# A hybrid attention and recurrence layer on one core: the last head's norm taken for both halves at once, attention's first query products ahead of its transposes, and query and key copies ahead of their remainders

## The chip, the cores and the metric

The kernel runs on one core of one Trainium2 chip, in one launch. The metric is the time of one execution in microseconds (us); lower is better. The engines are called as in the profile: PE is the matrix engine (matmuls and transposes, results in the accumulation banks, PSUM), DVE the vector engine, ACT the scalar engine, POOL the general-purpose engine, and SP the engine whose queue issues most transfers. Each engine carries out its own instructions strictly in the order in which they were written down; between engines they wait on semaphores.

## The reference

One layer of a bidirectional encoder over 1024 tokens of width 1024 (plus 16 learned meta tokens), cut to what matters here:

```python
a = rms_norm(h, norm_mix[l])
(q_na, k_na, v_na, q_hg, z_f, z_b, i_hg, g_hg, gate_na, gate_hg) = split_cols(a @ w_in[l])
y_na = neighbourhood_attention(hd(q_na), hd(k_na), hd(v_na), na_rpb[l]).reshape(B, L, NA_WIDTH) @ w_na_out[l]
y_hg = hgrn2_branch(q_hg, z_f, z_b, i_hg, g_hg, lb_all[:, l], hg_norm[l]) @ w_hg_out[l]
mix = jax.nn.sigmoid(gate_na) * y_na + jax.nn.sigmoid(gate_hg) * y_hg
h = h + mix @ w_o[l]
...
# the end of hgrn2_branch: o is (B, L, heads, 128)
o = o * lax.rsqrt(jnp.mean(o * o, axis=-1, keepdims=True) + EPS)
o = o.reshape(B, L, HG_VDIM) * gain * jax.nn.silu(g)
...
# neighbourhood_attention: 8 heads of 64, a window of 8 x 16 tokens of the grid, and the meta keys
p = softmax([q . k_window * scale + bias, q . k_meta * scale]);  out = p . [v_window, v_meta]
```

## The kernel before

The layer runs as a sequence of stages on one core: the first norm and the transposition of the tokens (`start`), four heads of the recurrence (`hgrn`, one call for each head `hd`), four pairs of attention heads (the loop over `p`), the two gates and the two output projections, and the MLP. All products are made to near-float32 accuracy by splitting each operand into a rounded high part and a remainder (`hi` and `lo`): `mm3` issues three matmuls for one product, lines L122, L123 and L124, so a projection of 128 columns from 1024 features over 512 tokens is 8 x 3 = 24 matmuls.

`proj(col, evac, meta_evac)` makes one block of 128 columns of the input projection. For a query block it runs in two pieces of 512 tokens. For a key or value block (which also need the 16 meta tokens) it runs in three: 256 tokens, 256 tokens with the 16 meta tokens (272 columns), and 512 tokens. Each piece has an accumulation bank of its own, all named `mm` in the profile, and `evac` copies it out. `mm_tile` hands these banks out in a cycle of three: two from the pool `mm`, one from the pool `mx`. So a piece waits until the piece three places earlier has been copied out.

The end of a recurrence head stands behind the `yield` of `hgrn`. Its output lies in two accumulation banks `po`, one for each half of the tokens (`hf` = 1, then 0). For each half: ACT squares it (`sq`), DVE sums the squares (`ss`), POOL makes the reciprocal root in two instructions (`st`, `hrs`; helper `rsqrt_mean`, L92 and L93), DVE scales (`on`), PE transposes the four 128-blocks (`opt`, L490), DVE applies gain and gate (`ot`), and SP writes `ot` to memory. Before the change DVE does one half to its end before it begins the other.

Attention takes two heads of 64 as a pair, stacked in 128 partitions. `ev_q` copies a query piece into two tiles `QX0` and `QX1` (index `i`): ACT writes the rounded copy of head `i` into its 64 partitions (L749), DVE the remainder into the other 64 (L750). `ev_k` does so for the keys: ACT writes the rounded copy twice into `KS0` or `KS1` (L757 and, shifted by 64 partitions, L758), DVE the remainder into `KL0` or `KL1` (L759). `mev_k` does the same for the meta keys (L766 to L768). After the value projection come the scores (`nsc`, L799 and L800), their softmax (`pr`: DVE L805, ACT L807, DVE L808 and L809), the transposes of the probabilities (`ppt`, L820 and L822) copied out as `PT`, and the products with the values (`pov`). The projection matmuls of the next pair fill PE between them. Meanwhile POOL adds the bias into the mask (`NB`, L742) and makes sums of the tokens for a later stage (`rt`, L187 and L191).

The weight block of a projection is loaded into `raw`, and split by ACT into `hi` (L112, or L115 with a scale) and by DVE into `lo` (L113 or L116), one block ahead of its use. `hi` and `lo` have two buffers each.

The start of the layer is recorded in the order in which it is written (`manual_schedule`). From the first recurrence head to the end of the gates a scheduler sets the order on each engine, so the order on an engine can differ from the order of the source: it already moves the first query projection of attention in between the last head's products.

## Time and profile before

| | |
|---|---|
| time, median of 3 runs | 1529.9 us (1528.22 to 1530.62) |
| time of the profiled execution | 1530.97 us |
| its span from the first to the last instruction | 1529.2 us |
| PE busy in the span | 1503.1 us (98%) |
| DVE, ACT, POOL busy | 1034.4, 657.4, 377.6 us |
| the recurrence ends, attention begins | about 334 to 347 us from the start |
| the four attention pairs | about 343 to 576 us |

The profiled execution took 1.77 us more than its span, and 1.07 us more than the median. PE is busy nearly all the time, so what an edit can win is a stretch in which PE stands idle. A row of the timeline gives the start of an instruction and its duration in us, the engine, the line of the kernel, the operation, what it writes and reads, and the shapes; in square brackets stands how long the engine was idle before it and what ended that wait. Matmuls overlap: the next one starts before the modelled end of the last.

### The profile page before, as it was taken

What the parts mean: (1) busy time and instruction counts of PE and PEld (TensorE: products, weight loads), DVE (VectorE), ACT (ScalarE), POOL (GpSimd) and SP (SyncE); (2) the same over time, 40 slices, a digit from 0 to 9 for tenths busy, and PEclk for the clock granted to TensorE, in tenths of its full rate; (3) what the DMA queues carried; (4) which work ended last, traced back from release to release, by engine and by line L of the source; (5) the groups of instructions that cost most, each with busy time, mean ns of one, the idle gap of its engine ahead of it and who ended that gap; (6) DMA issues with size and microseconds to landing.
All of it is one profiled execution on the core that took longest, in us unless ns stands there. A gap on an engine that the chain in (4) does not pass through costs nothing.

```text
span 1529.2 us, 23532 instructions
## 1 busy us (share of the span) xinstructions
PE 1503.1 (98%) x9236; PEld 1255.8 (82%) x9236; DVE 1034.4 (68%) x1608; ACT 657.4 (43%) x1168; POOL 377.6 (25%) x355
## 2 busy tenths in 40 slices
PE   9999999999999999999999999999999999999998
PEld 8888888878888887887888887888888888888886
DVE  7876566645786777666475358877777544877876
ACT  6131313126665576334133235455555533434444
POOL 3313130324404400011000122444444200231142
PEclk9999999999999999999999999999999999999999
DMA  4201011113222227435756123544444576563324
GB/s 168 59 29 57 28 57 29 48 47 108 80 68 94 95 68 244 132 130 172 248 165 220 53 86 117 177 154 153 152 151 158 208 261 234 193 234 110 96 83 152
DMA packets 142591, 195.61 MB, mean 128 GB/s; under 512 B 8192, under 2 KB 90240, under 8 KB 142480
## 3 DMA queue, kind: packets, MB, share of 16 engines
q1 hardware_dynamic: 133216, 172.53, 34.3%
q10 hardware_dynamic: 7088, 14.24, 2.4%
q0 software_dynamic: 2176, 7.34, 1.3%
q8 instruction: 72, 1.18, 0.3%
q14 instruction: 39, 0.32, 0.1%
HBM read 139.56 MB, written 54.53 MB: 127 GB/s over the span
## 4 chain that ended last, share of the span: by engine, by line
PE 89%; DVE 5%; issue 2%; ACT 2%; DMA 1%; POOL 0%; POOLq 0%; ACTq 0%; SPq 0%; DVEq 0%
PE mm L122 11%; PE mm L123 10%; PE mm L124 10%; PE mm L1372 5%; PE pa L1372 4%; PE pb L879 4%; PE pb L880 4%; PE pb L881 4%; PE pb L1372 4%; PE pc L1372 4%; PE pc L879 3%; PE pc L881 3%; PE pc L880 3%; PE pa L879 2%; PE pa L880 2%
## 5 line engine op out<-in xcount | busy, mean ns | idle before, releaser
L122 PE MATMUL mm<-aT,hi 128*128 128x512 f32 (+2 forms) x600 | 214.7, 358 | 2.8 <-DVE QX L750 1.5
L124 PE MATMUL mm<-aT,lo 128*128 128x512 f32 (+2 forms) x600 | 212.2, 354 | 0.0
L123 PE MATMUL mm<-aT,hi 128*128 128x512 f32 (+2 forms) x600 | 211.2, 352 | 0.0
L97 DVE TENSOR_TENSOR dl<-ur,dh 128x1024 fp32r<-128x1024 f32 x54 | 71.1, 1316 | 87.3 <-ACT dh L96 85.3
L96 ACT CAST dh<-ur 128x1024 fp32r<-128x1024 f32 x54 | 56.9, 1054 | 166.4 <-issue 91.1
L122 PEld LDWEIGHTS mm<-aT,hi 128*128 128x128 f32 x600 | 113.2, 189 | 16.1 <-issue 1.7
L124 PEld LDWEIGHTS mm<-aT,lo 128*128 128x128 f32 x600 | 113.2, 189 | 12.5
L123 PEld LDWEIGHTS mm<-aT,hi 128*128 128x128 f32 x600 | 113.3, 189 | 11.7
L112 ACT CAST hi<-raw 128x1024 fp32r<-128x1024 f32 x34 | 35.7, 1051 | 97.1 <-PE mm L123 68.4
L1177 DVE TENSOR_TENSOR wl<-raw,wh 128x512 fp32r<-128x512 f32 x50 | 41.0, 822 | 36.4 <-ACT wh L1176 36.3
L1181 ACT ACTIVATE uv<-uv 128x512 f32<-128x512 f32 x48 | 30.4, 633 | 80.1 <-DVE uv L1289 48.9
L1177 DVE TENSOR_TENSOR wl<-sx,wh 128x512 fp32r<-128x512 f32 x70 | 61.1, 883 | 3.4 <-ACT wh L1176 3.3
L1176 ACT CAST wh<-sx 128x512 fp32r<-128x512 f32 x70 | 42.1, 619 | 42.2 <-PE pc L880 23.9
L1462 POOL TENSOR_TENSOR w<-w,tt 128x512 f32<-128x512 f32 x16 | 23.4, 1461 | 132.9 <-DVE tt L1461 113.2
L300 POOL TENSOR_TENSOR Y<-X,TN 128x512 f32<-128x512 f32 x20 | 34.3, 1713 | 84.7 <-DVE X L297 84.7
L805 DVE CUSTOM_DVE_ANT_0 pr<-nsc,NB 128x432 f32<-128x432 f32 (+1 forms) x64 | 35.2, 559 | 26.7 <-PE nsc L800 26.4
L113 DVE TENSOR_TENSOR lo<-raw,hi 128x1024 fp32r<-128x1024 f32 x34 | 46.1, 1357 | 8.5 <-ACT hi L112 8.4
L409 DVE TENSOR_TENSOR QQ<-QQ,TN 128x512 f32<-128x512 f32 x48 | 35.1, 741 | 22.9 <-PE sc L404 22.9
L879 PE MATMUL pb<-nt,wh 128*128 128x512 f32 x128 | 50.2, 392 | 0.4 <-DVE uv L1259 0.2
L122 PE MATMUL mm<-wh,mT 128*128 128x512 f32 x128 | 50.2, 392 | 0.0
L124 PE MATMUL mm<-wh,mT 128*128 128x512 f32 x128 | 50.0, 390 | 0.0
L880 PE MATMUL pb<-nt,wh 128*128 128x512 f32 x128 | 49.9, 390 | 0.0
(408 smaller groups left out, 4445.8 us busy)
## 6 DMA issues: line engine op xcount, KB each, us to landing
raw<-in_w_in SPq DMA_DIRECT2D x56, 512.0 KB, 4.1
ur<-usp SPq DMA_DIRECT2D x54, 512.0 KB, 3.6
raw<-in_w_up SPq DMA_DIRECT2D x16, 1024.0 KB, 6.1
usp<-us SPq DMA_DIRECT2D x60, 256.0 KB, 2.3
sg<-gsp SPq DMA_DIRECT2D x16, 512.0 KB, 4.0
w<-in_w_dn SPq DMA_DIRECT2D x16, 512.0 KB, 4.8
usp<-uv SPq DMA_DIRECT2D x30, 256.0 KB, 2.8
gsp<-gv ACTq DMA_DIRECT2D x24, 256.0 KB, 2.8
```

Of the source, the lines that this page charges most:

```text
L96: act.copy(hi, src)
L97: dve.tensor_tensor(lo, src, hi.bitcast(F32), op=ALU.subtract)
L113: dve.tensor_tensor(lo[:, :kc], raw[:, :kc], hi[:, :kc].bitcast(F32), op=ALU.subtract)
L122: pe.matmul(ps, lh, rh, start=first, stop=False)
L123: pe.matmul(ps, lh, rl, start=False, stop=False)
L124: pe.matmul(ps, ll, rh, start=False, stop=last)
L879: pe.matmul(ps, lhs[0][:, c], rhs[0][:, k], start=first and k == 0, stop=False, skip_group_check=True)
L880: pe.matmul(ps, lhs[0][:, c], rhs[1][:, k], start=False, stop=False, skip_group_check=True)
L881: pe.matmul(ps, lhs[1][:, c], rhs[0][:, k], start=False, stop=k == 3, skip_group_check=True)
L1176: act.copy(v(hi), src)
L1177: dve.tensor_tensor(v(lo), src, v(hi).bitcast(F32), op=ALU.subtract)
L1372: pe.matmul(ps, a[n == 2][:, q, j * P:(j + 1) * P], b[n == 1][:, q], start=first and n == 0, stop=last and n == 2, skip_group_check=True)
```

## The change

Three edits, and one that goes with them.

1. In `hgrn`, the end of a head first makes the squares, sums and reciprocal roots of both halves, then scales both, then transposes both.
2. A new function `first_query` makes the two pieces of attention's first query block. Its first piece is written ahead of the last head's end and its second behind it, in the two `mm` banks; the whole part up to the keys of the first pair is recorded in the order of the source on PE, ACT and DVE. The cycle of banks is turned around (`mm_cycle`), so that the first key piece takes the bank of the first query piece, and the second key piece takes `mx`.
3. `ev_q` and `ev_k` make the rounded copies of both heads first and the remainders behind them. The shifted second copy of the keys now reads the first copy instead of the accumulation bank, and comes last.

```diff
         list(more)
         yield
+        rss = {}
         for hf in (1, 0):
-            po = pos[hf]
             sq = tmp("sq").rearrange("p (c v) -> p c v", v=P)
-            act.activation(sq, po, AF.Square)
+            act.activation(sq, pos[hf], AF.Square)
             ss = hp.tile([P, 4], F32, tag="ss", name="ss", bufs=2)
             dve.tensor_reduce(ss, sq, axis=AX.X, op=ALU.add)
             st = hp.tile([P, 4], F32, tag="st", name="st", bufs=2)
-            rs = hp.tile([P, 4], F32, tag="hrs", name="hrs", bufs=2)
-            rsqrt_mean(rs, ss, P, st)
-            on = tmp("on").rearrange("p (c v) -> p c v", v=P)
-            dve.tensor_tensor(on, po, fap(rs, 0, [[1, 4], [0, P]]), op=ALU.mult)
+            rss[hf] = hp.tile([P, 4], F32, tag="hrs", name="hrs", bufs=2)
+            rsqrt_mean(rss[hf], ss, P, st)
+        ons = {}
+        for hf in (1, 0):
+            ons[hf] = tmp("on").rearrange("p (c v) -> p c v", v=P)
+            dve.tensor_tensor(ons[hf], pos[hf], fap(rss[hf], 0, [[1, 4], [0, P]]), op=ALU.mult)
+        for hf in (1, 0):
             pt = bank("a", "opt")
             for c in range(4):
-                pe.transpose(pt[:, c], on[:, c], ident)
+                pe.transpose(pt[:, c], ons[hf][:, c], ident)
...
+    def first_query():
+
+        hi, lo = block_of(C_QN)
+        early[C_KN] = block_of(C_KN)
+        for h in range(2):
+            ps = bank("mm", "mm").rearrange("p a b -> p (a b)")
+            for k in range(KC):
+                mm3(ps, hi[:, k], lo[:, k], *(t[:, k, :TH] for t in aT[h]), k == 0, k == KC - 1)
+            yield ps
+    in_order = ExitStack()
+    in_order.enter_context(tc.manual_schedule(engines={e.engine for e in (pe, act, dve)}))
+    query = first_query()
+    query_ps = [next(query)]
     list(prev)
+    query_ps += list(query)
     hps.close()
...
     psum_pools(mx=1, s=2, t=2, b=1)
+    mm_cycle[1:] = mm_cycle[:0:-1]
...
             def ev_q(ps, t0, n):
                 for i in range(2):
+                    act.copy(strips(QX[i], 64 * i, t0, n), grid(ps, 64 * i))
+                for i in range(2):
                     b = 64 * i
-                    hi = strips(QX[i], b, t0, n)
-                    act.copy(hi, grid(ps, b))
-                    dve.tensor_tensor(strips(QX[i], 64 - b, t0, n), grid(ps, b), hi.bitcast(F32), op=ALU.subtract)
-            proj(C_QN + p * P, ev_q)
+                    dve.tensor_tensor(strips(QX[i], 64 - b, t0, n), grid(ps, b),
+                                      strips(QX[i], b, t0, n).bitcast(F32), op=ALU.subtract)
+            if p == 0:
+                for h in range(2):
+                    ev_q(query_ps[h], h * TH, TH)
+            else:
+                proj(C_QN + p * P, ev_q)
 
             def ev_k(ps, t0, n):
                 for i in range(2):
+                    act.copy(strips(KS[i], 64 * i, t0, n), grid(ps, 64 * i))
+                for i in range(2):
                     b = 64 * i
-                    hi = strips(KS[i], b, t0, n)
-                    act.copy(hi, grid(ps, b))
-                    act.copy(strips(KS[i], 64 - b, t0, n), grid(ps, b))
-                    dve.tensor_tensor(strips(KL[i], b, t0, n), grid(ps, b), hi.bitcast(F32), op=ALU.subtract)
+                    dve.tensor_tensor(strips(KL[i], b, t0, n), grid(ps, b),
+                                      strips(KS[i], b, t0, n).bitcast(F32), op=ALU.subtract)
+                    act.copy(strips(KS[i], 64 - b, t0, n), strips(KS[i], b, t0, n).bitcast(F32))
...
             proj(C_KN + p * P, ev_k, mev_k)
+            in_order.close()
```

The order of the built programs shows where instructions really move. The rows give line, operation, what is written and read (with the tile's number), and the shape. On POOL and SP nothing changes place, and on PE nothing but the following.

On PE, at the end of the last head, before: behind the last product of the head (`po`) stand the transposes of the first half, then the last three matmuls of the first query piece (`mm_4025`), the first nine of the second (`mm_4054`, three of them shown), and then the transposes of the other half.

```order
L474 MATMUL po_3920<-SB_3844,QQ_3245 128x128
L490 MATMUL opt_3943<-ident_77,on_3941 128x128 x4
L122 MATMUL mm_4025<-aT00_87,hi_3650 128x512
L123 MATMUL mm_4025<-aT01_88,hi_3650 128x512
L124 MATMUL mm_4025<-aT00_87,lo_3651 128x512
...
L122 MATMUL mm_4054<-aT10_89,hi_3650 128x512
L123 MATMUL mm_4054<-aT11_90,hi_3650 128x512
L124 MATMUL mm_4054<-aT10_89,lo_3651 128x512
L490 MATMUL opt_3961<-ident_77,on_3959 128x128 x4
```

On PE at the same place now (`mm_3941` is the first query piece, `mm_4002` the second):

```order
L474 MATMUL po_3920<-SB_3844,QQ_3245 128x128
L122 MATMUL mm_3941<-aT00_87,hi_3650 128x512
L123 MATMUL mm_3941<-aT01_88,hi_3650 128x512
L124 MATMUL mm_3941<-aT00_87,lo_3651 128x512
L493 MATMUL opt_3986<-ident_77,on_3982 128x128 x4
L493 MATMUL opt_3994<-ident_77,on_3984 128x128 x4
L122 MATMUL mm_4002<-aT10_89,hi_3650 128x512
```

Only three query matmuls stand ahead of the transposes now, and the nine that stood between the two halves stand behind both.

On DVE, from there to the first key piece, before (`lo_4086` is the remainder of the first value block's weights):

```order
L482 TENSOR_REDUCE ss_3935<-sq_3933 128x4
L487 TENSOR_TENSOR on_3941<-po_3908,hrs_3938 128x512
L492 SCALAR_TENSOR_TENSOR ot_3948<-opt_3943,gain_sb_84,gs_3312 128x512
L482 TENSOR_REDUCE ss_3953<-sq_3951 128x4
L487 TENSOR_TENSOR on_3959<-po_3920,hrs_3956 128x512
L492 SCALAR_TENSOR_TENSOR ot_3966<-opt_3961,gain_sb_84,gs_3312 128x512
L113 TENSOR_TENSOR lo_4086<-raw_4083,hi_4085 128x1024
L750 TENSOR_TENSOR QX0_3995<-mm_4025,QX0_3995 64x8x64
L750 TENSOR_TENSOR QX0_3995<-mm_4054,QX0_3995 64x8x64
L750 TENSOR_TENSOR QX1_3996<-mm_4025,QX1_3996 64x8x64
L750 TENSOR_TENSOR QX1_3996<-mm_4054,QX1_3996 64x8x64
```

And now:

```order
L482 TENSOR_REDUCE ss_3968<-sq_3966 128x4
L482 TENSOR_REDUCE ss_3976<-sq_3974 128x4
L489 TENSOR_TENSOR on_3982<-po_3908,hrs_3971 128x512
L489 TENSOR_TENSOR on_3984<-po_3920,hrs_3979 128x512
L495 SCALAR_TENSOR_TENSOR ot_3991<-opt_3986,gain_sb_84,gs_3312 128x512
L495 SCALAR_TENSOR_TENSOR ot_3999<-opt_3994,gain_sb_84,gs_3312 128x512
L769 TENSOR_TENSOR QX0_4053<-mm_3941,QX0_4053 64x8x64
L769 TENSOR_TENSOR QX1_4054<-mm_3941,QX1_4054 64x8x64
L769 TENSOR_TENSOR QX0_4053<-mm_4002,QX0_4053 64x8x64
L769 TENSOR_TENSOR QX1_4054<-mm_4002,QX1_4054 64x8x64
L113 TENSOR_TENSOR lo_4088<-raw_4085,hi_4087 128x1024
```

The second sum stands ahead of the first scaling, both remainders of the first query piece stand ahead of those of the second, and the weights' remainder moved behind all four. ACT moves in the same way: the four query copies now stand ahead of the weights' high part (`hi`, L112), behind which they stood before.

On ACT, at the end of a pair, where the next pair's query copies stand between the last two exponentials of this one (the names behind `waits` are the engines that an instruction waits for), before:

```order
L831 CAST PT0_4522<-ppt_4578 128x128 [waits DVE_49]
L807 ACTIVATE pr_4605,sm_4607<-pr_4605,mn_4606 128x432 [waits DVE_49,Activation_49]
L807 ACTIVATE pr_4625,sm_4627<-pr_4625,mn_4626 128x288 [waits DVE_49,Activation_49]
L749 CAST QX1_3996<-mm_4691 64x8x64 [waits DVE_49,PE_49]
L831 CAST PT0_4613<-ppt_4615 128x4x128 [waits PE_49,Activation_49]
```

And now:

```order
L857 CAST PT0_4525<-ppt_4581 128x128 [waits DVE_49]
L766 CAST QX1_4054<-mm_4694 64x8x64 [waits PE_49]
L833 ACTIVATE pr_4608,sm_4610<-pr_4608,mn_4609 128x432 [waits DVE_49,Activation_49]
L833 ACTIVATE pr_4628,sm_4630<-pr_4628,mn_4629 128x288 [waits DVE_49,Activation_49]
L857 CAST PT0_4616<-ppt_4618 128x4x128 [waits PE_49,Activation_49]
```

The copy of the second head moved ahead of the two exponentials, and no longer waits for DVE.

## The prediction

> **What bounds the kernel now.** I read the page first, for the share of PE.
>
> ```profile
> span 1529.2 us, 23532 instructions
> PE 89%; DVE 5%; issue 2%; ACT 2%; DMA 1%; POOL 0%; POOLq 0%; ACTq 0%; SPq 0%; DVEq 0%
> ```
>
> PE makes up 89% of the chain that ended last, so a microsecond on another engine counts only where PE stands still for it. Next I read who kept PE waiting (columns: who waited for whom, total us, times, longest).
>
> ```profile
> PE opt L490 <- DVE on L487: 1.7, 2, 0.9
> PE ppt L820 <- DVE pr L809: 1.5, 3, 0.5
> PE mm L122 <- DVE QX L750: 1.5, 1, 1.5
> PE mm L122 <- DVE KL L759: 1.3, 2, 0.6
> ```
>
> The change touches the first, third and fourth of these directly: 4.5 us, or 0.3% of the span, are all it can take away there. Now the timeline, at the end of the last head.
>
> ```profile
> 333.62 0.39 PE L474 MATMUL po<-SB,QQ 128*128 128x128 f32 x2
> 334.04 0.60 ACT L480 ACTIVATE sq<-po 128x512 f32<-128x512 f32 x1 [2.08 <-PE po L474]
> 334.10 0.69 DVE L487 TENSOR_TENSOR on<-po,hrs 128x512 f32<-128x512 f32 x1 [1.42 <-POOL hrs L93]
> 334.84 0.65 PE L490 MATMUL opt<-ident,on 128*128 128x128 f32 x4 [0.84 <-DVE on L487]
> 335.54 0.75 DVE L492 SCALAR_TENSOR_TENSOR ot<-opt,gain_sb,gs 128x512 f32<-128x512 f32 x1 [0.75 <-PE opt L490]
> 336.20 0.68 DVE L482 TENSOR_REDUCE ss<-sq 128x4 f32<-128x512 f32 x1
> 338.29 0.69 DVE L487 TENSOR_TENSOR on<-po,hrs 128x512 f32<-128x512 f32 x1 [1.41 <-POOL hrs L93]
> 339.12 0.63 PE L490 MATMUL opt<-ident,on 128*128 128x128 f32 x4 [0.89 <-DVE on L487]
> 339.51 0.48 PE L122 MATMUL mm<-aT,hi 128*128 128x512 f32 x1
> 343.02 0.28 PE L122 MATMUL mm<-aT,hi 128*128 128x256 f32 x1
> 343.04 1.05 ACT L112 CAST hi<-raw 128x1024 fp32r<-128x1024 f32 x1 [8.40 <-PE mm L123]
> 343.99 1.05 ACT L749 CAST QX<-mm 64x512 fp32r<-64x512 f32 x2
> 344.12 1.23 DVE L113 TENSOR_TENSOR lo<-raw,hi 128x1024 fp32r<-128x1024 f32 x1 [3.58 <-ACT hi L112]
> 345.37 2.02 DVE L750 TENSOR_TENSOR QX<-mm,QX 64x512 fp32r<-64x512 f32 x3
> 345.77 0.28 PE L124 MATMUL mm<-aT,lo 128*128 128x256 f32 x1
> 347.55 0.36 PE L122 MATMUL mm<-aT,hi 128*128 128x272 f32 x1 [1.49 <-DVE QX L750]
> ```
>
> PE waits at 334.84 and 339.12 for the scaled output of one half each. The third wait is the odd one: at 347.55 the second key piece needs the bank of the first query piece, whose matmuls ended soon after 335. Its copies had not run, because ACT stood from 335 to 343.04 at the cast of the next weights, which wanted a weight buffer that the query matmuls still read. The remainders on DVE then came behind `lo` as well.
>
> **Part 1, the norm of both halves.** The head's last product starts at 333.62. The three matmuls that now follow take about 0.23 each: fifteen from 339.51 to 343.02 make (343.02 − 339.51)/15 = 0.234. PE is through with them near 334.4. DVE now makes the second sum first: it needs the square (334.04 + 0.60 = 334.64), takes 0.69, and ends near 335.35. Only then comes the first scaling, to 336.06, and the transposes start at 336.11 instead of 334.84. The second half's root runs on POOL meanwhile: the sum of 336.20 to 336.88 led to a scaling at 338.29, 1.41 later, so the second scaling starts at 335.35 + 1.41 = 336.76 and ends at 337.45. With the 0.14 seen from 338.98 to 339.12, the second transposes start near 337.57, and with the 0.39 from there to 339.51 the second query piece starts at 337.96. Its 24 matmuls take 24 × 0.234 = 5.62, to 343.58; before, this point was 343.02. So the norm alone loses 0.56: the two waits are no longer filled by the nine matmuls that stood between them.
>
> **Part 2, the query products and the banks.** ACT's casts of the first query piece start behind the second square, at 334.65. Two take 1.05 + 0.1, so DVE can subtract as soon as it is through with the gains, which end about 1.5 (two of 0.75) after the second scaling, at 338.97; two remainders (three took 2.02, so 1.35) are done at 340.4. The first key piece wants that bank at 343.58, so it does not wait, with 3.2 to spare. The second key piece takes `mx`, and in the built order its first matmul waits for nothing; the third takes the second query bank: its casts run from 343.8 to 344.9, its remainders to 346.3, and it is wanted near 349.5. The first key piece takes as long as before, from 343.02 to its last matmul at 345.77 and 0.12 to the next slot: 2.87. The second key piece so starts at 343.58 + 2.87 = 346.45, where it started at 347.55: **1.10 gained**, the 0.56 lost already in it. What moved behind the queries is the weights' `hi` and `lo` of the first value block: about 2 later, near 347.5, and wanted when that block starts, behind 24 matmuls at 0.13 and 24 at 0.234, near 355; if POOL slows `lo` to the 2.81 shown below, it is still some 6 early. The next `raw` transfer on SP waits for that `lo` and slips by as much, and its block is multiplied only among the pair's scores, behind all three value pieces. SP and POOL are passed by nothing; the head's last `ot` is ready 1.6 earlier, and nobody near waits for it.
>
> **Part 3, the copies.** The two waits for `KL` are alike; here is the first in full and the row of the second.
>
> ```profile
> 471.12 2.81 DVE L116 SCALAR_TENSOR_TENSOR lo<-raw,hi 128x1024 fp32r<-128x1024 f32 x1 [2.14 <-ACT hi L115]
> 473.34 1.73 POOL L191 TENSOR_TENSOR rt<-rt 128x512 f32<-128x512 f32 x1
> 473.96 0.68 DVE L759 TENSOR_TENSOR KL<-mm,KS 64x512 fp32r<-64x512 f32 x1
> 474.68 0.58 ACT L757 CAST KS<-mm 64x512 fp32r<-64x512 f32 x1 [2.40 <-DVE KL L759]
> 475.27 0.58 ACT L758 CAST KS<-mm 64x512 fp32r<-64x512 f32 x1
> 475.69 0.28 PE L123 MATMUL mm<-aT,hi 128*128 128x272 f32 x1
> 475.81 0.29 PE L124 MATMUL mm<-aT,lo 128*128 128x272 f32 x1
> 475.89 0.69 DVE L759 TENSOR_TENSOR KL<-mm,KS 64x512 fp32r<-64x512 f32 x1 [1.24 <-ACT KS L758]
> 476.73 0.47 PE L122 MATMUL mm<-aT,hi 128*128 128x512 f32 x1 [0.63 <-DVE KL L759]
> 534.17 0.47 PE L122 MATMUL mm<-aT,hi 128*128 128x512 f32 x1 [0.64 <-DVE KL L759]
> ```
>
> `lo` took 2.81 while POOL worked, where it took 1.23 at 344.12. Behind it the two remainders could follow each other, but between them stood two copies of ACT, 474.68 to 475.85, which had waited for the first remainder. With both rounded copies made first, the second remainder ends at 473.96 + 0.68 + 0.71 = 475.35. PE's next slot is 475.81 + 0.12 = 475.93 instead of 476.73. **0.80 at each place, 1.6 together**, with a margin of 0.6 should `lo` run longer. The shifted copy now reads the first copy in SBUF. No row shows that; the cast of `hi` at 343.04 reads SBUF at 1.05 for 1024 columns, 0.53 for 512, against 0.58 from the bank, so between a little faster and, with a start-up of its own, some 0.2 slower. Taken as equal: the scores that need it come behind the three value pieces, so either way PE does not see it.
>
> In return, at the end of each of the first three pairs:
>
> ```profile
> 394.12 0.30 PE L800 MATMUL nsc<-KL,QX 128*128 128x288 f32 x1
> 394.39 0.24 ACT L831 CAST PT<-ppt 128x128 fp32r<-128x128 f32 x1
> 395.01 0.66 ACT L807 ACTIVATE pr<-pr,mn 128x432 f32<-128x432 f32 x1 [0.37 <-DVE rc L808]
> 396.01 0.68 DVE L750 TENSOR_TENSOR QX<-mm,QX 64x512 fp32r<-64x512 f32 x1
> 400.96 0.41 PE L820 MATMUL ppt<-ident,pr 128*128 128x128 f32 x2 [0.52 <-DVE pr L809]
> ```
>
> The query copy of 0.58 now precedes the exponential of 395.01. It may start when the last scores are done (394.12 + 0.30 = 394.42) and ACT is free (394.63), so the exponential begins at 395.23, 0.2 later. What follows it on DVE ends in the scaling that PE waits for at 400.96, so no more than 0.2 reaches PE, and none of it, or even a gain, if ACT, which is rid of the copy later on, makes it up. The waits for `pr` are three, one for each of these pairs: I take 0.1 each, nearer to the loss since PE already waits, **0.3 lost**.
>
> **The sum.** 1.1 + 1.6 − 0.3 = 2.4 us less, against the profiled execution's 1530.97 (its span is 1529.2): 1528.6. That execution was 1.07 above the median of the runs shown, so the median goes from 1529.9 to **1527.5**, 0.16% less. PE stays in its order behind these places, and the transfers behind them are released by the same work, so I expect the gain to reach the end. A change under 0.2% (3.1 us) can hardly be told from none here.
>
> **Rivals.** One wait that I left out is PE's longest, at the end of attention.
>
> ```profile
> 575.51 0.88 PE L820 MATMUL ppt<-ident,pr 128*128 128x128 f32 x3 [2.35 <-DVE PT L832]
> 575.00:580.00 5.00, 4.49 (x17) 3.83 (x18) 4.58 (x8) 3.10 (x8) 0.00 (x0) 0.66 0.74 250
> 343.00:348.00 5.00, 3.51 (x29) 3.31 (x28) 3.50 (x5) 3.84 (x7) 2.15 (x3) 1.00 1.03 336
> ```
>
> These are the wait and two windows (the third number from the end is the granted clock). Behind the wait of 2.35 the clock was 0.66 of full over 5 us, which costs 0.34 × 5 = 1.7; behind the 1.49 at 347.55 it was 1.00.
>
> *The slow stretch at 575 goes.* If that wait shortens, or falls differently, 1.7 more is won: 1527.5 − 1.7 = 1525.8. Nothing in the change acts there but what comes before it is moved. Chance 0.2.
>
> *The norm gets a slow stretch of its own; the change does not do what it says.* The two waits of part 1 (334.4 to 336.11 and 336.5 to 337.57, together 2.8) now have only four transposes between them. If they count as one, 1.7 is lost there and 0.7 is left: 1529.2. The longer one, 1.7, is nearer to the 1.49 that kept the clock than to 2.35. Chance 0.15. [...]
>
> *The query copy holds up the exponentials.* If the copy moved ahead on ACT still starts only behind the first head's remainder (396.01 + 0.68 = 396.69), the exponential starts at 397.3 instead of 395.01, and DVE, which has no slack, passes 2.3 on to PE. Three pairs make 6.9 against the 2.7 gained elsewhere: 4.2 slower, 1534.1. It decides from 0.9 per pair on. Against it: the order shows that the copy no longer waits for DVE. Chance 0.05.
>
> The forecast itself has 0.5, between 1526.2 and 1528.8; the remaining 0.1 is for shifts of `lo` against POOL elsewhere, either way by about 1.6 (2.81 − 1.23) a place.
>
> **The numbers.** Faster by over 0.2% (below 1526.8) are nearly the whole of the first rival, a quarter of the forecast and half of the rest: 0.18 + 0.13 + 0.04 = 0.35. Slower by over 0.2% (above 1533.0) are the third rival's upper part and little else: 0.05. The rest, 0.60, is within. The range reaches from the lower side of the first rival, 1524.8, to the upper side of the second, 1530.6.
>
> **What would show it.** Right: no wait ahead of the second key piece; the `opt` waits near 1.7 and 1.0, longer than before; no `KL` wait; `QX` casts near 334.7. Wrong: a clock below 1.00 between 335 and 345, an exponential that waits behind a query copy, `ppt` waits above 0.8, or a `lo` of 2.8 where it was 1.2.

## The result, and the profile after

The changed kernel takes 1527.73 us (median of 21 runs, 1526.46 to 1529.57); the kernel before, run beside it, 1530.73 us (21 runs, 1528.22 to 1532.85). The ratio is 0.9983 with a 95% interval of 0.9977 to 0.9989: 2.6 us less, between 1.7 and 3.5 (the medians differ by 3.0). The profiled execution took 1527.06 us. One of the executions behind the table further below, of the kernel called "changed, copies undone", took 5304.65 us; it counts in that kernel's median, but not in its ratio.

From the page of the changed kernel: its span, and the engines' shares of the chain that ended last.

```profile
span 1525.3 us, 23529 instructions
PE 86%; DVE 5%; issue 3%; POOL 3%; ACT 2%; DMA 1%; SPq 0%; POOLq 0%; ACTq 0%; DVEq 0%
```

PE still carries the chain, so its waits are again what is to be compared. Here is the list of them between 330 and 580 us (who waited for whom, total us, times, longest; gaps of about 0.1 are not in it).

```profile
PE ppt L846 <- DVE PT L858: 2.4, 1, 2.4
PE opt L493 <- DVE on L489: 2.2, 2, 1.3
PE ppt L846 <- DVE pr L835: 1.3, 3, 0.6
PE nsc L825 <- DVE mn L831: 1.0, 2, 0.5
```

The wait for `QX` and the two for `KL` are gone. Those for the norm grew from 1.7 to 2.2, and those for `pr` fell from 1.5 to 1.3. All listed waits of PE in this stretch fell from 9.4 to 6.9.

The start of attention in the timeline of the changed kernel:

```profile
334.36 0.39 PE L474 MATMUL po<-SB,QQ 128*128 128x128 f32 x2
335.47 1.17 ACT L766 CAST QX<-mm 64x512 fp32r<-64x512 f32 x2
336.75 0.66 PE L493 MATMUL opt<-ident,on 128*128 128x128 f32 x4 [1.31 <-DVE on L489]
338.25 0.65 PE L493 MATMUL opt<-ident,on 128*128 128x128 f32 x4 [0.84 <-DVE on L489]
339.72 1.39 DVE L769 TENSOR_TENSOR QX<-mm,QX 64x512 fp32r<-64x512 f32 x2
344.20 0.28 PE L122 MATMUL mm<-aT,hi 128*128 128x256 f32 x1
347.07 0.29 PE L122 MATMUL mm<-aT,hi 128*128 128x272 f32 x1
```

The two waits at the transposes now end 1.5 apart, with nothing but four transposes (0.66) between them. The first query piece is copied out by 341.11 (339.72 + 1.39), long before the first key piece wants its bank at 344.20, and the second key piece starts at 347.07 without a wait. Where the change begins, this execution runs 0.74 behind the one before (334.36 against 333.62). Taken from there, the first key piece comes 0.44 later than before (344.20 − 334.36 = 9.84, where it was 343.02 − 333.62 = 9.40), and the second 1.22 earlier (12.71, where it was 13.93).

The keys' copies of the third pair, where PE waited at 476.73 before, and in the last row the same place of the fourth pair (534.17 before):

```profile
470.71 1.19 ACT L779 CAST KS<-mm 64x512 fp32r<-64x512 f32 x2
470.72 2.75 DVE L116 SCALAR_TENSOR_TENSOR lo<-raw,hi 128x1024 fp32r<-128x1024 f32 x1 [2.93 <-ACT hi L115]
471.81 1.26 ACT L784 CAST KS<-KS 64x512 fp32r<-64x512 f32 x2
473.50 1.39 DVE L782 TENSOR_TENSOR KL<-mm,KS 64x512 fp32r<-64x512 f32 x2
475.54 0.40 PE L122 MATMUL mm<-aT,hi 128*128 128x512 f32 x1
531.98 0.40 PE L122 MATMUL mm<-aT,hi 128*128 128x512 f32 x1
```

All four copies of ACT are done before DVE is through with `lo`; the two remainders follow each other (1.39 for both), and PE goes on at 475.54 with no wait, as it does at 531.98.

The same run at the end of attention: the longest wait, and two windows (the third number from the end is the granted clock).

```profile
573.14 0.52 PE L846 MATMUL ppt<-ident,pr 128*128 128x128 f32 x3 [2.35 <-DVE PT L858]
335.00:340.00 5.00, 2.84 (x16) 1.96 (x15) 3.66 (x6) 1.53 (x3) 3.62 (x6) 1.00 0.07 24
575.00:580.00 5.00, 5.00 (x28) 4.23 (x27) 4.97 (x9) 3.52 (x7) 0.00 (x0) 1.00 0.59 168
```

The wait of 2.35 is as long as before, but this time the clock stayed at 1.00 behind it. PE reaches it at 573.14 instead of 575.51; less the 0.74 of the late start that is 3.11 us gained by the work of the change. The spans differ by 3.9 since the profile before also has the slow stretch behind its wait and this one has none. That second part isn't the change's: see below.

### The profile page after: what moved, and what is told of

The parts are those of the page before. It is cut to its first block, busy times and chain, and to the rows that moved or that the text cites. A ratio compares the mean times of both kernels' runs of the same rounds, so it can differ in the third digit from the quotient of the medians.

```text
span 1525.3 us, 23529 instructions
## 1 busy us (share of the span) xinstructions
PE 1501.0 (98%) x9236; PEld 1254.6 (82%) x9236; DVE 1035.1 (68%) x1608; ACT 657.7 (43%) x1168; POOL 378.5 (25%) x355
## 4 chain that ended last, share of the span: by engine, by line
PE 86%; DVE 5%; issue 3%; POOL 3%; ACT 2%; DMA 1%; SPq 0%; POOLq 0%; ACTq 0%; DVEq 0%
PE mm L122 10%; PE mm L123 10%; PE mm L124 9%; PE mm L1398 5%; PE pa L1398 4%; PE pb L905 4%; PE pb L906 4%; PE pb L907 4%; PE pb L1398 4%; PE pc L1398 4%; PE pc L905 3%; PE pc L907 3%; PE pc L906 3%; PE pa L905 2%; PE pa L906 2%
## 5 line engine op out<-in xcount | busy, mean ns | idle before, releaser
L112 ACT CAST hi<-raw 128x1024 fp32r<-128x1024 f32 x34 | 35.7, 1051 | 88.3 <-PE mm L123 78.1
L122 PE MATMUL mm<-wh,mT 128*128 128x512 f32 x128 | 50.2, 392 | 0.0
L907 PE MATMUL pb<-nt,wl 128*128 128x512 f32 x128 | 49.8, 389 | 0.0
```

Of the source, the lines that this page charges most:

```text
L122: pe.matmul(ps, lh, rh, start=first, stop=False)
L907: pe.matmul(ps, lhs[1][:, c], rhs[0][:, k], start=False, stop=k == 3, skip_group_check=True)
```

## The experiments

Each kernel was timed beside the kernel before, with 5 to 11 executions (21 of the changed one); the ratio is to the executions of before that ran beside it. The column "to the keys" is the time from the last `po` product to the first key piece; "waits" is the sum of PE's waits from 330 us to the end of the fourth pair; "slow at the norm" says whether the profile shows a stretch of reduced clock behind the transposes.

| kernel | median us | ratio to before, 95% | to the keys | waits | slow at the norm |
|---|---|---|---|---|---|
| before | 1530.73 | 1 | 9.40 | 9.4 | no |
| changed | 1527.73 | 0.9983 (0.9977 to 0.9989) | 9.84 | 6.9 | no |
| copies only | 1527.27 | 0.9976 (0.9967 to 0.9985) | 9.40 | 6.6 | no |
| changed, copies undone | 1529.77 | 0.9995 (0.9986 to 1.0004) | 11.47 | 7.8 | yes |
| norm only | 1529.01 | 0.9988 (0.9979 to 0.9997) | 7.90 | 7.4 | no |
| changed, cycle kept | 1527.37 | 0.9980 (0.9971 to 0.9989) | 11.44 | 6.3 | yes |
| key copies only | 1527.08 | 0.9981 (0.9972 to 0.9990) | 9.40 | 7.6 | no |
| query copies only | 1529.26 | 0.9991 (0.9982 to 1.0000) | 9.38 | 7.7 | no |
| changed, key copy from the bank | 1528.74 | 0.9994 (0.9985 to 1.0003) | 9.84 | 6.5 | no |
| changed, weights first | 1534.59 | 1.0027 (1.0016 to 1.0037) | 15.39 | 10.1 | yes |
| changed, all queries ahead | 1526.95 | 0.9980 (0.9971 to 0.9989) | 10.00 | 6.9 | no |
| norm and copies | 1524.84 | 0.9963 (0.9951 to 0.9976) | 7.89 | 5.5 | no |
| changed, twelve queries ahead | 1524.20 | 0.9957 (0.9944 to 0.9971) | 7.28 | 4.4 | no |
| the last, bias later | 1522.77 | 0.9947 (0.9934 to 0.9961) | 7.28 | 2.3 | no |

### Copies only

Part 3 alone, in the kernel before; for the queries (`ev_k` goes as in the change):

```diff
                 for i in range(2):
+                    act.copy(strips(QX[i], 64 * i, t0, n), grid(ps, 64 * i))
+                for i in range(2):
                     b = 64 * i
-                    hi = strips(QX[i], b, t0, n)
-                    act.copy(hi, grid(ps, b))
...
```

> The kernel before with only the new order of the query and key copies; norm and query products as before. Theory (the edits pay where PE waited, each by itself): both waits on KL near 476.7 and 534.2 (0.63 + 0.64) are gone; the two waits on opt stay at 0.84 and 0.89; the second key piece still waits for QX near 347.5, by 1.0 to 1.5, since ACT's cast of the next weights still stands ahead of the query casts; the three ppt waits hold 1.3 to 1.6 together. PE is 1.3 to 1.6 us earlier at the end of the fourth pair than before. Time 1529 to 1529.5 us, ratio 0.9988 to 0.9993. Rival (the copies won nothing that lasts, the gain is all at the start of attention): PE is 0.3 or less earlier at the end of the pairs, ratio 0.9998 to 1.0002.

Rows of this kernel's timeline, one ahead of the second key piece and one of the third pair:

```profile
345.77 2.82 DVE L750 TENSOR_TENSOR QX<-mm,QX 64x512 fp32r<-64x512 f32 x4
471.69 1.39 DVE L759 TENSOR_TENSOR KL<-mm,KS 64x512 fp32r<-64x512 f32 x2
```

They show the first theory's picture: no `KL` wait, and ahead of the second key piece a `QX` wait that fell from 1.49 to 0.9, since the remainders of the first piece are now the first two of the four on DVE (345.77 and half of 2.82 make 347.18; PE goes on at 347.31). But the gain is twice what I expected: 0.9976, and 3.31 us ahead at the end of the fourth pair (572.60 against 575.51, and 0.40 late at the start). Part 3 by itself is worth at least as much as the whole change. So parts 1 and 2 together must be worth about nothing.

### Copies undone: parts 1 and 2 alone

```diff
                 for i in range(2):
-                    act.copy(strips(QX[i], 64 * i, t0, n), grid(ps, 64 * i))
-                for i in range(2):
                     b = 64 * i
+                    hi = strips(QX[i], b, t0, n)
+                    act.copy(hi, grid(ps, b))
...
```

> The changed kernel with the query and key copies in their old order; norm and query products as changed. Theory: the opt waits are those of the changed kernel (together 2.2), the QX wait ahead of the second key piece stays away (0 to 0.3), the two KL waits come back at 0.5 to 0.7 each. PE is about 1.2 us earlier than before at the second key piece and 1.1 earlier at the end of the pairs. Time 1529 to 1530 us, ratio 0.9990 to 0.9996. Rival (the QX wait went because of the order of the copies): a QX wait of 0.5 or more is back ahead of the second key piece, ratio 0.9998 to 1.0002.

The `QX` wait stays away and PE waits again at both places of the key copies, as the theory has it: 0.60 for `KL` in the third pair, and 0.58 in the fourth, where ACT's copy `vT` ended after `KL`. The ratio is 0.9995, and its interval includes 1. The profile, taken of a long execution (1531.98), shows where the 1.2 us can get lost: the first key piece comes 11.47 behind the last product, not 9.84, with the same two waits (1.31 and 0.85). Behind them stands a stretch of reduced clock (0.84 of full over 335 to 340 us and 0.82 over 340 to 345). I show it on the next kernel but one.

### Norm only

Part 1 alone, in the kernel before; its core:

```diff
+        for hf in (1, 0):
+            ons[hf] = tmp("on").rearrange("p (c v) -> p c v", v=P)
+            dve.tensor_tensor(ons[hf], pos[hf], fap(rss[hf], 0, [[1, 4], [0, P]]), op=ALU.mult)
+        for hf in (1, 0):
             pt = bank("a", "opt")
```

> The kernel before with only the norm written for both halves at once; the scheduler still sets the order on PE, so query products stand between and behind the two groups of transposes. Theory (the 0.4 to 0.6 that the changed kernel loses at the norm is the lost filling, not the norm itself): the two opt waits are together 1.7 or less, the first key piece starts within 0.3 of where it did, the QX wait of 1.5 and the KL waits of 0.6 stay; ratio 0.9995 to 1.0005. Rival (the norm for both halves costs by itself, since both sums stand ahead of the first scaling): opt waits of 2.2 or more, the first key piece 0.4 to 0.6 later, ratio 1.0002 to 1.0006.

The timeline of this kernel:

```profile
336.54 0.39 PE L474 MATMUL po<-SB,QQ 128*128 128x128 f32 x2
337.76 0.66 PE L493 MATMUL opt<-ident,on 128*128 128x128 f32 x4
340.54 0.63 PE L493 MATMUL opt<-ident,on 128*128 128x128 f32 x4 [0.27 <-DVE on L489]
344.44 0.28 PE L122 MATMUL mm<-aT,hi 128*128 128x256 f32 x1
```

The scheduler put four query products ahead of the first transposes and eight between the two groups. One wait of 0.27 is left of 1.73, and the first key piece comes 7.90 behind the last product, 1.5 earlier than before. So the norm for both halves is a gain by itself, which neither theory had expected. What costs in the changed kernel is the fixed order, with three products ahead of the transposes and none between.

### The cycle of banks kept

```diff
-    mm_cycle[1:] = mm_cycle[:0:-1]
```

> The changed kernel with the cycle of banks in its old direction: the pieces of the first keys take the banks in the other order. Theory (the turn of the cycle is nearly idle: the second query bank is copied out at 346.99, and the second key piece starts at 347.07): at most 0.1 us of wait ahead of the second key piece, none elsewhere that the changed kernel has not; ratio to before 0.9977 to 0.9989, as the changed kernel. Rival (the turn of the cycle is what took the QX wait away): a QX wait of 0.5 to 1.5 ahead of a key piece, ratio 0.9987 to 0.9995.

The time is that of the changed kernel, and no wait for `QX` is back: the turn of the cycle is idle. The profile fell on the slow kind of norm. Rows of PE, then the two windows:

```profile
338.08 1.12 PE L493 MATMUL opt<-ident,on 128*128 128x128 f32 x4 [0.84 <-DVE on L489]
339.43 0.63 PE L123 MATMUL mm<-aT,hi 128*128 128x512 f32 x1
339.85 0.63 PE L124 MATMUL mm<-aT,lo 128*128 128x512 f32 x1
335.00:340.00 5.00, 2.85 (x13) 2.15 (x12) 3.38 (x5) 1.37 (x3) 3.78 (x6) 0.80 0.10 36
340.00:345.00 5.00, 5.00 (x21) 4.04 (x20) 1.38 (x2) 0.00 (x0) 0.92 (x1) 0.86 0.79 248
```

Behind the second wait a query product follows the last after 0.42 (339.43 to 339.85) instead of 0.23. The two windows lose (0.20 + 0.14) × 5 = 1.7 us; the first key piece comes 1.60 later than in the profile of the changed kernel (11.44 against 9.84) with waits of the same length. Of the five profiles in which the transposes wait 1.31 and 0.84 or 0.85 (changed, copies undone, cycle kept, key copy from the bank, weights first) three show this stretch. Of the nine others none does, whether their waits lie apart (0.84 and 0.87 to 0.89, 3.4 us between them) or are filled.

### Key copies only, query copies only

Part 3 in halves, each in the kernel before: first `ev_k` alone, then `ev_q` alone (its diff is that of "copies only").

```diff
                 for i in range(2):
+                    act.copy(strips(KS[i], 64 * i, t0, n), grid(ps, 64 * i))
+                for i in range(2):
...
-                    act.copy(strips(KS[i], 64 - b, t0, n), grid(ps, b))
...
+                    act.copy(strips(KS[i], 64 - b, t0, n), strips(KS[i], b, t0, n).bitcast(F32))
```

> The kernel before with the new order in the key copies alone. Theory (the KL waits are made by the key copies alone, the QX wait and the ppt waits by the query copies): the two KL waits of 0.63 and 0.64 are gone, worth 0.8 each with the slower first matmul behind a stop; the QX wait stays at 1.4 to 1.5, the three ppt waits at 1.4 to 1.6 together; PE 1.5 to 1.8 us ahead of before at the end of the fourth pair; ratio 0.9985 to 0.9993. Rival (the whole part 3 hangs on the keys): 3 us ahead there, ratio 0.9975 to 0.9982.

> The kernel before with the new order in the query copies alone. Theory: the two KL waits stay at 0.6 each; the QX wait ahead of the second key piece falls from 1.49 to about 0.9, since DVE now makes both remainders of the first piece before anything of the second; the ppt waits fall from 1.5 to 1.1 or less together, since ACT and DVE no longer take turns at the end of a pair; PE 1.2 to 1.6 us ahead at the end of the fourth pair, ratio 0.9988 to 0.9994. Rival (the query copy moved ahead of the exponential delays the softmax, as the forecast took it): the ppt waits grow to 1.7 or more together, ratio 0.9995 to 1.0005.

The keys alone come to 0.9981 and are 2.64 ahead at the end of the fourth pair, between what the two theories expected; the queries alone come to 0.9991 and 1.19. The `KL` waits hang on the key copies and the `QX` wait on the query copies (1.49 with the first, 0.86 with the second), as the theory said. The `ppt` waits didn't grow with the query copies: 0.8 together. The surplus of the keys lies at the end of the second pair, where this profile has no wait for `pr` at all. The rows show DVE's last scaling of the pair and POOL's addition of the bias into the mask, before:

```profile
456.62 2.46 POOL L742 TENSOR_TENSOR NB<-NB,bs 128x384 f32<-128x384 f32 x3 [29.69 <-DMA NB<-in_wmask]
456.77 1.01 DVE L809 TENSOR_SCALAR pr<-pr,rc 128x288 f32<-128x288 f32 x1
```

in the changed kernel:

```profile
456.21 2.46 POOL L761 TENSOR_TENSOR NB<-NB,bs 128x384 f32<-128x384 f32 x3 [29.93 <-DMA NB<-in_wmask]
456.23 1.15 DVE L835 TENSOR_SCALAR pr<-pr,rc 128x288 f32<-128x288 f32 x1
457.53 0.41 PE L846 MATMUL ppt<-ident,pr 128*128 128x128 f32 x2 [0.58 <-DVE pr L835]
```

and with the key copies only:

```profile
457.41 0.35 DVE L810 TENSOR_SCALAR pr<-pr,rc 128x288 f32<-128x288 f32 x1
457.87 2.41 POOL L742 TENSOR_TENSOR NB<-NB,bs 128x384 f32<-128x384 f32 x3 [30.27 <-DVE pr L810]
```

The same scaling takes 0.35 where it begins ahead of POOL's addition and 1.01 or 1.15 where POOL is 0.15 or 0.02 ahead. In these two cases it ends 1.16 and 1.17 behind POOL's start: one of POOL's three additions (2.46/3 = 0.82) and then 0.35. That reads as if DVE stood still for POOL's first addition, and PE waited for DVE. The last experiment tests it.

### The shifted key copy from the bank

```diff
-                    act.copy(strips(KS[i], 64 - b, t0, n), strips(KS[i], b, t0, n).bitcast(F32))
+                    act.copy(strips(KS[i], 64 - b, t0, n), grid(ps, b))
```

> The changed kernel, with the shifted key copy read from the accumulation bank again instead of from the first copy in SBUF. Theory (the source of that copy is of no account: 0.41 from SBUF against 0.37 from the bank for 256 columns, and nobody waits for it): no new wait of PE above 0.2; ratio to before 0.9977 to 0.9989, as the changed kernel. Rival (the copy from SBUF frees the bank earlier, and that is worth something): a wait for KS ahead of a projection piece, ratio 0.9985 to 0.9995.

Rows of its timeline, at the keys of the third pair:

```profile
472.58 0.68 DVE L782 TENSOR_TENSOR KL<-mm,KS 64x512 fp32r<-64x512 f32 x1
473.30 0.58 ACT L784 CAST KS<-mm 64x512 fp32r<-64x512 f32 x1 [2.34 <-DVE KL L782]
473.91 0.69 DVE L782 TENSOR_TENSOR KL<-mm,KS 64x512 fp32r<-64x512 f32 x1 [0.65 <-ACT KS L784]
475.30 0.50 PE L122 MATMUL mm<-aT,hi 128*128 128x512 f32 x1 [0.54 <-ACT KS L784]
```

The rival is right here. Read from the bank, the copy waits 2.34 for the first remainder, the second remainder waits 0.65 for the copy, and PE waits 0.54 for the last copy. By the end of attention it is 2.40 ahead of before instead of 3.11. The ratio is 0.9994 (0.9985 to 1.0003), above that of the changed kernel, with a small overlap of the intervals. The 0.7 of the trace are less than the ratios differ by, 1.7 us; the medians, each against its own before, differ by 1.2, and two long executions (1532.54 and 1533.29) weigh on the ratio. The rest stays open. The source matters not by its duration (0.63 from SBUF, half of the 1.26 shown above, against 0.58) but because it takes ACT out of the bank on which DVE works.

### Weights first

```diff
+                early[C_VN] = block_of(C_VN)
                 for h in range(2):
                     ev_q(query_ps[h], h * TH, TH)
```

> The changed kernel, with the cast and the remainder of the first value weights (hi, lo) written ahead of the query copies again. Theory (the QX wait came from ACT standing at that cast for a weight buffer that the query products still read, with the query copies behind it): the cast starts only when the second query piece is done, near 344, the query copies follow near 345, and the first key piece, which takes the first query bank, waits for QX by 3 to 4 us; time 1530 to 1531.5, ratio 0.9997 to 1.0007. Rival (the turned cycle of banks and the early first piece are enough by themselves): no QX wait above 0.5, ratio 0.9977 to 0.9989.

The cast of the weights and the first key piece in its timeline:

```profile
345.49 1.04 ACT L112 CAST hi<-raw 128x1024 fp32r<-128x1024 f32 x1 [10.41 <-PE mm L123]
349.45 0.55 PE L122 MATMUL mm<-aT,hi 128*128 128x256 f32 x1 [3.81 <-DVE QX L769]
```

ACT stood 10.41 at the cast of the weights, and PE then waited 3.81 for the query copies behind it, as the theory had it. The cause of the old `QX` wait is shown. The time is 3 us above my figure: this profile has the slow stretch at the norm (0.79 of full over 335 to 340 us and 0.87 over 340 to 345) and another one behind the 3.81 (0.81 over 345 to 350, 0.51 over 350 to 355).

### More filling: all queries ahead, twelve queries ahead, and norm with copies

With all 24 matmuls of the second query piece ahead of the transposes (`KC` is 8, one step is 3 matmuls):

```diff
-            yield ps
+                yield ps
...
-    query_ps = [next(query)]
+    query_ps = [next(query) for _ in range(KC + 8)]
...
-    query_ps += list(query)
+    query_ps = (query_ps + list(query))[::KC]
```

> The changed kernel with the whole second query piece (24 matmuls) ahead of the transposes. Theory (more filling than the norm takes only delays the rest): no opt waits, but the transposes start near 340 instead of 336.75, the gains (ot) end near 341.5, and the remainders of the first query piece stand behind them on DVE, so that the first key piece, wanted near 341, waits for its bank by 1 to 3 us; ratio 0.9970 to 0.9985, that is 1 to 2 us longer than with twelve matmuls ahead. Rival (the order behind the norm doesn't matter to PE): no wait above 0.3 ahead of the key pieces, the same time as with twelve ahead, ratio 0.9965 to 0.9972.

The transposes, the query remainders and the first key piece:

```profile
340.82 1.03 PE L493 MATMUL opt<-ident,on 128*128 128x128 f32 x8
342.90 2.11 DVE L769 TENSOR_TENSOR QX<-mm,QX 64x512 fp32r<-64x512 f32 x3
344.44 0.36 PE L122 MATMUL mm<-aT,hi 128*128 128x256 f32 x1 [2.58 <-DVE QX L769]
```

No wait at the norm, but one of 2.58 behind it: the gains, and with them the query remainders on DVE, come too late for the bank. With twelve ahead and twelve behind (the other lines as above):

```diff
-    query_ps = [next(query)]
+    query_ps = [next(query) for _ in range(KC + 4)]
```

> The changed kernel, but the second query piece is made in two parts: its first twelve matmuls are written ahead of the transposes of the last head's norm, the other twelve behind them. Theory (the two opt waits of 2.15 are lost filling, and nothing else hangs on them): twelve matmuls by 0.23 make 2.7, so the opt waits shrink to 0.3 or less together; the distance from the last po product to the first key piece falls from 9.84 to about 7.8; no QX wait; no stretch of reduced clock between 335 and 345. Time 1525.2 to 1526, ratio to before 0.9965 to 0.9972, 1.5 to 2.2 us less than the changed kernel. Rival (a wait moves: with the norm filled the second key piece comes 2 us earlier and meets its bank or its weights too early): a wait of 1 or more ahead of a key piece, ratio 0.9977 to 0.9985.

The transposes and the first two key pieces:

```profile
338.23 1.04 PE L493 MATMUL opt<-ident,on 128*128 128x128 f32 x8
341.84 0.36 PE L122 MATMUL mm<-aT,hi 128*128 128x256 f32 x1
344.79 0.29 PE L122 MATMUL mm<-aT,hi 128*128 128x272 f32 x1
```

PE waits for nothing from 334.56 (the last product) to the second key piece. The keys come 2.56 earlier than in the changed kernel, and the time is 1524.20, ratio 0.9957, still less than the 1525.2 I expected. By the wait of 2.35 it is 2.44 ahead of the changed kernel (236.34 from the last product, where that has 238.78). The medians differ by 3.5. Behind attention the two profiles show where the rest can come from: near 595 PE waits 0.33 for the cast of weights where the changed kernel waits 1.10, and near 711 it hardly waits for `gv` where the changed kernel waits 0.53, which makes PE 0.74 and 0.39 earlier. Whether the stretch of reduced clock, which has no wait of the norm left to follow (the clock is 1.00 over 335 to 345 us in this profile), has a part in it too was not measured. The same was tried without writing an order: the edits of "norm only" and "copies only" together, in the kernel before.

> The kernel before with the norm for both halves and the new order of the copies, without the query products written out ahead: the scheduler sets their order. Measured apart, the norm took the distance from the last po product to the first key piece from 9.40 to 7.90, and the copies were 3.3 us ahead at the end of the fourth pair. Theory (the two are independent): opt waits 0.4 or less together, a QX wait of 0.7 to 1.2 ahead of the second key piece, no KL wait; 4.5 to 5 us ahead of before at the end of the fourth pair; time 1525.5 to 1526.5, ratio 0.9967 to 0.9975, so below the changed kernel. Rival (the query products ahead of the transposes are worth having, since they alone take the QX wait away): the time is that of the changed kernel or longer, ratio 0.998 or more.

It comes to 1524.84, with a `QX` wait of 0.86 left; it is 4.06 ahead at the end of the fourth pair, less than the 4.5 to 5 expected. So the order written by hand in part 2 isn't needed for the gain; without twelve products ahead it loses what the scheduler gives.

### The bias later

On top of twelve ahead:

```diff
+            sp.dma_start(NB[:, :, :1008], wmask.unsqueeze(1).broadcast_to([P, 2, 1008]))
             for i in range(2):
...
-                sp.dma_start(NB[:, i, :1008], wmask)
```

> The kernel with twelve query matmuls ahead of the transposes, and the mask of a pair (NB) loaded for both heads in one transfer instead of two, so that it lands later and POOL's addition of the bias starts later. In the profiles so far DVE's last scaling of a pair (pr, 128x288) took 0.35 where it began before that addition, and 0.70 to 1.15 where POOL began first; DVE then ended 1.16 to 1.25 behind POOL's start. Theory (the three ppt waits are that collision): POOL starts 1 to 2 us later, the three scalings take 0.35, the ppt waits, 1.2 together, fall to 0.2 or less; 1.0 to 1.6 us less than with twelve ahead alone: time 1522.5 to 1523.3, ratio 0.9946 to 0.9954. Rival (the waits are set by DVE's own order, the long scaling only fills time in which DVE would wait): the ppt waits stay at 0.9 or more, ratio 0.9957 or more.

The end of the first pair on DVE and POOL, a remainder of weights among the scores of the second pair, and a wait of PE in a later stage with the cast that stands ahead of it:

```profile
397.36 0.35 DVE L835 TENSOR_SCALAR pr<-pr,rc 128x288 f32<-128x288 f32 x1
398.32 3.40 POOL L761 TENSOR_TENSOR NB<-NB,bs 128x384 f32<-128x384 f32 x4 [29.12 <-DMA NB<-in_wmask]
422.67 1.22 DVE L113 TENSOR_TENSOR lo<-raw,hi 128x1024 fp32r<-128x1024 f32 x1
705.18 1.05 ACT L96 CAST hi<-raw 128x1024 fp32r<-128x1024 f32 x1 [2.02 <-DMA raw<-in_w_hg]
708.14 0.50 PE L905 MATMUL pb<-at,hi 128*128 128x512 f32 x1 [1.83 <-DVE gv L998]
```

At all three ends of pairs the scaling takes 0.35 and PE doesn't wait for it; of the listed waits between 330 us and the end of the fourth pair only the last, 2.35, is left. From the last product to that wait it is 2.59 us less than with twelve ahead alone (233.75 against 236.34). That is more than the 1.0 to 1.6 expected, since the wait of 0.79 at the scores of the second pair is gone as well. With twelve ahead alone the remainder `lo` that stands ahead of it on DVE is long:

```profile
422.97 2.29 DVE L113 TENSOR_TENSOR lo<-raw,hi 128x1024 fp32r<-128x1024 f32 x1
```

POOL began an addition of its sums `rt` there at 422.90, just ahead of `lo`. Here it began at 420.92 and was over, after 1.29, before `lo` began, and `lo` took 1.22. This is the same picture as at the ends of the pairs.

About 1.8 is given back at 708, where PE waits for `gv`, which it hardly does with twelve ahead alone. DVE's `gv` stands behind a remainder there, the remainder behind ACT's cast of 705.18, and that cast waited 2.02 for a transfer of weights (1.23 with twelve ahead alone). Why the transfer came later was not tested. Waits for `gv` at this place, of 0.5 to 1.7, are also in five profiles whose bias is not moved, the one before among them (1.19). The median still falls by 1.4, to 1522.77, ratio 0.9947: below before by 8 us and below the changed kernel by 5. That is more than these two profiles leave of the gain, and the difference stays open.

## Why the prediction was right, step by step

The time (1527.5 against 1527.73) came out, and the sum before the clock is close: 2.4 forecast, 3.11 seen by the end of attention. The forecast counted from a median of 1529.9 for the kernel before, which came out at 1530.73 beside the changed one, so the gain is a little larger than forecast: 2.6 by the ratio. Not all terms came about as described, and one event that I gave 0.15 happens in part of the executions.

- **The norm alone loses 0.56.** It lost 0.44 (9.84 against 9.40). The transposes start 2.39 and 3.89 behind the last product; 2.49 and 3.95 were forecast. The waits themselves are shorter than forecast, 1.31 and 0.84 instead of 1.7 and 1.0, since PE was through with the three query products 1.08 behind the last product (336.75 − 1.31 − 334.36) and not 0.8. The order of events was right, `ss` ahead of the first scaling included. The reason given, lost filling, is shown: with the filling kept (norm only) the norm wins 1.5, and with twelve products ahead the waits vanish.
- **No `QX` wait, second key piece 1.10 earlier.** It came 1.22 earlier. The cause named, ACT standing at the weights with the copies behind it, is shown by the kernel with the weights first (3.81). The turned cycle of banks has no part in it: without it nothing changes. The weights' `lo` behind the queries took 1.85 instead of 1.23, and PE did not wait for it.
- **The `KL` waits, 0.80 each.** They came out. PE's lead over the profile before, read at one and the same instruction of both, grows from 0.40 (457.93 against 457.53) to 1.19 (476.73 against 475.54) at the first place and from 1.41 (515.37 against 513.96) to 2.19 (534.17 against 531.98) at the second: 0.79 and 0.78. The forecast left out that the next matmul follows a stop after 0.30 instead of 0.23, another 0.07 each.
- **The shifted copy taken as equal.** Its duration was (0.63 against 0.58). "Either way PE does not see it" holds for that difference, but not for the source: from the bank a wait of 0.54 is back. What I had overlooked is that a third access of ACT to the bank stands between DVE's two.
- **0.3 lost at the ends of pairs.** The size came out, the way to it did not. The transposes of the first pair ahead of the wait for `pr`, before and in the changed kernel:

```profile
399.20 0.55 PE L820 MATMUL ppt<-ident,pr 128*128 128x128 f32 x3
398.97 0.55 PE L846 MATMUL ppt<-ident,pr 128*128 128x128 f32 x3
```

PE's lead is 0.40 at the matmul ahead of them (398.99 against 398.59), 0.23 at these transposes and 0.39 behind the wait. In the second pair it goes from 0.70 to 0.54 and 0.40, in the third from 1.37 to 1.21 and 1.41. So each pair loses 0.16 or 0.17 at the transposes, in a gap too short for the list of waits: DVE, whose `PT` they wait for, is that much later, as the exponentials are (the one behind the query copy starts 1.53 behind the one ahead of the copy, where it was 1.27 behind it). At the wait for `pr`, where I had put the loss, 0.16 is won back, 0.14 lost and 0.20 won. Together 0.27 is lost, all of it in the second pair (0.30); that the size fits is partly luck.

What I had wrong is what sets the wait for `pr`. The three waits went from 0.52, 0.44 and 0.54 to 0.35, 0.58 and 0.35. DVE's scaling did move back, by 0.16 in the second pair (456.77 − 450.77 = 6.00 before, 456.23 − 450.07 = 6.16 after, counted from an exponential of the same step), but the waits follow another thing: how long the scaling takes beside POOL. It went from 1.09, 1.01 and 1.11 to 0.93, 1.15 and 0.92, by −0.16, +0.14 and −0.19, and the waits by −0.17, +0.14 and −0.19. I had put the wait down to DVE's work ahead of the scaling; it was the scaling itself, stretched.

- **The gain reaches the end.** It does, though two later waits of PE changed: near 596 it waits 1.10 for the cast of weights, where it waited 0.23 before, and near 712 it waits 0.53 for `gv`, where it waited 1.19.
- **The rival of the slow stretch at 575.** It did go in the profile after, but not by the change: the wait of 2.35 (2.43 in one) stands in thirteen profiles, and a stretch of reduced clock follows it in six of them. It moves single executions, and nothing in the profiles says that it moves one median more than the other.
- **The rival of a slow stretch at the norm.** It is real: three of five profiles with the two waits together have it, and it costs 1.6 to 1.7. It is the likeliest reason why parts 1 and 2 alone come out at nothing (0.9995), though they win 1.2 where the clock holds; in the profile of that kernel the wait for `gv` is longer too, 1.57 instead of 1.19. I estimate that it takes some 0.8 us from the changed kernel's 3.1 if it comes in half of its executions (1.65/2); that leaves 2.3, near the 2.6 of the ratio.
- **The rival of the held-up exponentials** fell: no exponential stands behind a remainder.

So the sum was too small by 0.7. Of that 0.12 lies at the second key piece and 0.2 in the matmuls behind the three stops that went; the waits at the scores add 0.1, and 0.3 is spread over steps of less than 0.1. The slow stretch at the norm, which the forecast had only as a rival, takes about as much by the estimate above. That the number fits so well is partly luck.

## What to carry to other kernels

Two short waits were cheaper apart here, with work between them, than side by side: with 0.84 and 0.87 to 0.89, 3.4 us apart, none of four profiles has a stretch of reduced clock behind them, with 1.31 and 0.84 or 0.85, four transposes apart, three of five have one. Before the same step is done for both halves at once, count the matmuls that are left to stand in the waits, and leave about as many as the waits are long (here twelve of 0.23 for 2.15, and both waits went). Where two engines copy one bank out, let one be through with it before the other begins (the two `KL` waits of 0.63 and 0.64 went), and take a further copy from where the first one lies (from the bank a wait of 0.54 was back). When an engine is waited for, compare the duration of its last instructions with the same instructions elsewhere: if one is two or three times as long, the thing to move is what runs beside it (here the scaling took 0.92 to 1.15 beside POOL's addition and 0.35 ahead of it, and with the addition later PE didn't wait for it).

## What was not expected of the hardware

- Between executions of nearly the same program the same wait was or was not followed by a stretch of reduced clock: 2.35 us (2.43 in one) in six of thirteen profiles, 1.31 and 0.84 or 0.85 with four transposes between in three of five, 1.49 in none of the three that have it. It followed the one wait of 3.81, and did not follow the one of 2.58. In the profile before the granted clock is 0.52 from 575.50 to 579.00 and 1.00 behind that, which costs 0.48 × 3.5 = 1.7 us. What decides when it comes is not shown.
- One DVE scaling of 128x288 took 0.35 where it began ahead of POOL's addition (0.05 ahead in "copies only") and 0.70 to 1.15 where POOL began first, with as little as 0.02 us between them. In the second case DVE ended 1.16 to 1.25 behind POOL's start.
